# First modulation sums two tiles at a time, one statistic product, and x loaded into the slots of the residual sums

## The chip, the cores and the metric

The kernel runs on one core of a Trainium2 chip. The metric is device time in microseconds (us); smaller is better. The core's engines are TensorE (PE; its weight loads are shown as PEld), VectorE (DVE), ScalarE (ACT), GpSimd (POOL) and SyncE (SP), which here only issues DMA transfers.

## What is computed

Two network blocks over 512 tokens of width 1024, in float32. Only the first matters here:

```python
c_act = jax.nn.silu(c)
mod = c_act @ ada_w[l] + ada_b[l]
shift, scale, gate = jnp.split(mod, 3, axis=-1)
h = rmsnorm(x, norm_g[l]) * (1.0 + scale[:, None, :]) + shift[:, None, :]
p = h @ w_in[l]
y_rwkv = rwkv7_group(p[..., :RWKV_COLS], ...)      # 8 heads
y_sb = stick_breaking_group(p[..., RWKV_COLS:], sb_norm_g[l])   # 8 heads
y = jnp.concatenate([y_rwkv, y_sb], axis=-1) @ w_out[l]
x = x + gate[:, None, :] * y
return rmsnorm(x, final_g)
```

The second block (a short convolution layer, then a neighbourhood attention layer, each with a feed-forward part, over these tokens and 256 context tokens) follows and is not touched.

## The kernel before

Activations lie feature by token: x is eight tiles of 128 features x 512 tokens. A float32 product with a weight is made of three fp32r products: each operand is split into a high part (a rounded copy, made on ACT) and a low part (the difference, made on DVE), and hi x hi, lo x hi and hi x lo are summed in PSUM (mm3, lines 172 to 174). A weight is loaded by SP into a slot "st" (two slots), split into wh and wl (lines 155 and 156; four slots each), and used. So an output tile of a product over six k tiles is 18 PE instructions, over eight 24.

**The head** (block1, lines 310 to 371). SP loads x as four pairs of tiles (512 KB each). The mean square of x (sumsq, lines 250 to 264) is made so: ACT squares the tiles, DVE adds the squares of tiles 0 to 5 into one, PE sums that over the features with a product by a constant matrix, and adds the squares of tiles 6 and 7 with two more such products; these are plain float32 products. Then rsqrt (lines 240 to 248): Ln and Exp on ACT. The modulation vector, shift and scale of all eight tiles, comes from c (cc, a small load on ACT's queue, then a tanh on ACT, line 331) and the 1024 x 2048 matrix ada_n, in four chunks of 512 columns. A chunk is loaded by SP in four transfers of two k tiles (512 KB, line 344). Each k tile is one product with a stationary operand of 32 columns, placed in one of four column groups of the array (line 348), so that four partial sums arise side by side in one PSUM bank. ACT copies the bank out (ev, line 350), four products with a selecting column add the four groups and turn the row into columns (line 353), and DVE adds the bias (line 356). Chunk 0 holds the scale of tiles 0 to 3, chunk 1 the shift of tiles 0 to 3, chunk 2 the scale and chunk 3 the shift of tiles 4 to 7. After a scale chunk the gain is made (line 359), after a shift chunk four tiles are modulated (modulate: nt on DVE at line 287, the high part h on ACT at 289, the low part on DVE at 290).

Between the chunks SP also loads the first halves (k tiles 0 to 3) of five weight tiles of w_in: 12 and 0 after chunk 1, 4 and 8 after chunk 2, 13 after chunk 3. Their products over k 0 to 3 start ahead, each in a PSUM bank of its own (banks ss, acc, acc, sc, so); those over k 4 to 7 follow when tiles 4 to 7 of h are there. "The five tiles" below are these.

**The middle.** Four pairs of RWKV heads (rwkv_pair) and four pairs of stick-breaking heads (sb_pair) are interleaved. An sb pair works through four query blocks of 128, two heads each: scores (line 1147), a mask (1148), two sigmoids on ACT (sg and om, 1151 and 1152), a running product on DVE (cum, 1156), a product (sg, 1158), transposes on PE (1162), a copy (pt, 1164), and products with v (so, 1169); then a norm (osq 1172, its product 1174, ors). Scores and transposes of all blocks share one PSUM bank (ss), so the eight steps of an sb pair are a chain. The modulation vectors of gate and of the next layers are made by DVE as a filler (line 210).

**Block 1's end** (lines 393 to 468). When the y tiles are there, each is split into h (lines 306 and 307, "split"), in the order YORD = (0, 4, 1, 5, 2, 6, 3, 7). Before the last two, the products with w_out over the first six (k 0 to 5) are made for eight outputs m: for m = 0 to 5 the sum "part" = x + gate * product is written over a slot of y that is free by then (lines 419 to 423), for m = 6 and 7 the product stays in PSUM. The bank "acc" has two slots, so the third product waits for the first part. The x tiles of these sums (xt, line 404) are loaded by SP into a pool "tail" that is opened after the last sb pair and lies over space of the RWKV pool; on SP's queue they stand ahead of the eight loads of the context (xc, line 407). The context is normed and modulated there as well (hc). Last come the products over the y tiles 3 and 7 (w_out2, line 448), the new x, and its statistics.

The order of the instructions on each engine's queue is not written out: a planner fixes it when the program is built, from the order in the text, priorities (high_priority raises one) and its own estimates of durations and transfers. On the chip each queue then runs in that order.

## Time and profile before

| | us |
|---|---|
| median of 3 runs | 2110.76 |
| lowest and highest of them | 2107.98, 2111.87 |
| profiled execution, its own time | 2105.49 |
| its span (first to last instruction) | 2103.7 |
| PE busy in it | 2051.8 |
| DVE busy | 1231.9 |
| ACT busy | 795.2 |

The profile shows one execution. A line of its timeline gives start, duration, engine, source line, operation and operands, and in brackets how long the engine was idle before and what ended that. A name before the arrow is what is written, those after it are read; "x5" counts instructions. "PEclk" is the clock that was granted to TensorE, as a share of full speed. PE's busy time is modelled and counts a product at a low clock as busy.

### The profile page before, as it was taken

To read this page: it belongs to the slowest core of one execution; us is meant where nothing else is said; L and a number is where in the kernel's file an instruction comes from. 1 tells how busy PE (TensorE), PEld (TensorE's weight loads), DVE (VectorE), ACT (ScalarE), POOL (GpSimd) and SP (SyncE) were. 2 spreads that over 40 slices of the span, in tenths; PEclk is the share of its full clock that TensorE was granted. 3 is DMA by queue.
4 is the path that set the end of the run, shared out by engine and by line. 5 is a ranking of instruction groups with operands and counts; after the bars stand their busy time and mean duration, and the time that the engine had idled before them with its cause. 6 is when DMAs were issued, how large, how long until landed. Compare 5 with 4: busy or idle time off the path is not lost.

```text
span 2103.7 us, 33543 instructions
## 1 busy us (share of the span) xinstructions
PE 2051.8 (98%) x13596; PEld 1651.6 (79%) x13596; DVE 1231.9 (59%) x2641; ACT 795.2 (38%) x1485; POOL 131.5 (6%) x212
## 2 busy tenths in 40 slices
PE   6999999998999999999999999999999999999999
PEld 3766666655888888888888888898777787888887
DVE  2969887645777756767456443354566655434443
ACT  3536444345422224221222122244777744323232
POOL 0000000000000000001001000000233200000000
PEclk9999999987999999999999999999999999999999
DMA  7432313112243421445234322222111122333333
GB/s 279 147 111 83 111 53 98 40 56 81 71 129 122 130 81 45 147 127 174 90 123 155 114 91 60 61 81 71 43 59 61 36 66 92 95 100 96 94 99 102
DMA packets 61356, 203.60 MB, mean 97 GB/s; under 512 B 6928, under 2 KB 8976, under 8 KB 61200
## 3 DMA queue, kind: packets, MB, share of 16 engines
q1 hardware_dynamic: 45360, 145.77, 21.3%
q0 software_dynamic: 15120, 55.06, 8.1%
q8 instruction: 107, 1.75, 0.3%
q10 hardware_dynamic: 720, 0.62, 0.1%
q14 instruction: 49, 0.40, 0.1%
HBM read 199.32 MB, written 2.10 MB: 96 GB/s over the span
## 4 chain that ended last, share of the span: by engine, by line
PE 87%; ACT 3%; DVE 3%; issue 1%; POOL 0%; POOLq 0%; ACTq 0%; DVEq 0%
PE acc L173 19%; PE acc L172 19%; PE acc L174 19%; PE cacc L174 5%; PE cacc L173 5%; PE cacc L172 5%; PE py L895 2%; PE pT L875 2%; PE ss L1147 1%; PE so L1169 1%; PE sm L862 1%; PE py L1083 1%; PE sm L863 1%; PE py L1081 1%; PE ss L1162 1%
## 5 line engine op out<-in xcount | busy, mean ns | idle before, releaser
L155 ACT CAST wh<-st 128x512 fp32r<-128x512 f32 (+2 forms) x481 | 292.3, 609 | 729.8 <-PE acc L173 287.7
L156 DVE TENSOR_TENSOR wl<-st,wh 128x512 fp32r<-128x512 f32 (+2 forms) x481 | 323.1, 674 | 353.9 <-ACT wh L155 350.7
L172 PE MATMUL acc<-xzzh,wh 128*128 128x512 f32 x352 | 138.8, 394 | 0.0
L174 PE MATMUL acc<-xzzh,wl 128*128 128x512 f32 x352 | 138.1, 392 | 0.0
L173 PE MATMUL acc<-xzzl,wh 128*128 128x512 f32 x352 | 138.0, 392 | 0.0
L210 DVE CUSTOM_DVE_ANT_0 junk<-ast,cb,vec 128x512 bf16<-128x512 f32 x168 | 125.2, 745 | 14.5 <-DMA ast<-in_w_ada_dram 11.9
L210 DVE CUSTOM_DVE_ANT_0 junk<-ast,cb,m 128x512 bf16<-128x512 f32 x168 | 125.5, 747 | 2.8
L200 POOL DMA_DIRECT2D ast<-in_w_ada_dram x96 | 50.6, 528 | 1022.3 <-DVE m L210 957.2
L174 PEld LDWEIGHTS acc<-xzzh,wl 128*128 128x128 f32 x352 | 66.0, 188 | 14.8
L172 PEld LDWEIGHTS acc<-xzzh,wh 128*128 128x128 f32 x352 | 66.1, 188 | 13.6 <-issue 0.5
L173 PEld LDWEIGHTS acc<-xzzl,wh 128*128 128x128 f32 x352 | 66.1, 188 | 13.4 <-issue 0.5
L172 PE MATMUL acc<-h0h,wh 128*128 128x512 f32 (+1 forms) x164 | 65.8, 401 | 6.0 <-DVE part L421 3.1
L173 PE MATMUL cacc<-czzl,wh 128*128 128x256 f32 x240 | 68.1, 284 | 0.0
L172 PE MATMUL cacc<-czzh,wh 128*128 128x256 f32 x240 | 67.7, 282 | 0.0
L174 PE MATMUL cacc<-czzh,wl 128*128 128x256 f32 x240 | 67.3, 280 | 0.0
L174 PE MATMUL acc<-h2h,wl 128*128 128x512 f32 (+1 forms) x164 | 65.8, 401 | 0.0
L173 PE MATMUL acc<-h1l,wh 128*128 128x512 f32 (+1 forms) x164 | 65.7, 401 | 0.0
L173 PE MATMUL acc<-h3l,wh 128*128 128x512 f32 (+1 forms) x164 | 65.3, 398 | 0.3 <-DVE h3l L290 0.3
L173 PE MATMUL acc<-h6l,wh 128*128 128x512 f32 (+1 forms) x164 | 65.5, 399 | 0.1
L173 PE MATMUL acc<-h0l,wh 128*128 128x512 f32 (+1 forms) x164 | 65.4, 399 | 0.0
L174 PE MATMUL acc<-h0h,wl 128*128 128x512 f32 (+1 forms) x164 | 65.3, 398 | 0.1
L174 PE MATMUL acc<-h1h,wl 128*128 128x512 f32 (+1 forms) x164 | 65.2, 398 | 0.0
(731 smaller groups left out, 5576.1 us busy)
## 6 DMA issues: line engine op xcount, KB each, us to landing
ast<-in_w_ada_dram POOLq DMA_DIRECT2D x96, 512.0 KB, 3.8
st<-in_ffn_w_in_dram SPq DMA_DIRECT2D x88, 512.0 KB, 3.4
st<-in_ffn_w_out_dram SPq DMA_DIRECT2D x32, 448.0 KB, 3.3
st<-in_w_in_dram SPq DMA_DIRECT2D x24, 512.0 KB, 3.5
st<-in_conv_w_in_dram SPq DMA_DIRECT2D x24, 512.0 KB, 3.6
ast<-in_ada_n_dram SPq DMA_DIRECT2D x16, 512.0 KB, 9.0
st<-in_ffn_w_out_dram SPq DMA_DIRECT2D x16, 512.0 KB, 3.5
st<-in_w_qk_dram SPq DMA_DIRECT2D x16, 512.0 KB, 3.5
```

Of the source, the lines that this page charges most:

```text
L155: nc.scalar.copy(hi[:, :n], sl)
L156: nc.vector.tensor_tensor(lo[:, :n], sl, hi[:, :n].bitcast(F32), ALU.subtract)
L172: mm(out, lhsT=lh, rhs=rh, start=first, stop=False)
L173: mm(out, lhsT=lh, rhs=rl, start=False, stop=False)
L174: return mm(out, lhsT=ll, rhs=rh, start=False, stop=last)
L200: self.nc.gpsimd.dma_start(st, src)
L210: i = self.nc.vector.tensor_tensor_reduce(out=junk, in0=st[:, hs], in1=c[:, hs], scale=0.5, scalar=o if hf else self.V(bname, j), op0=ALU. ...
L862: mm(o, lhsT=qh[:, e, qs], rhs=ks, start=True, stop=False)
L863: mm(o, lhsT=ql[:, e, qs], rhs=ks, start=False, stop=True)
L875: nc.tensor.transpose(pT[:, to], s[:, 128 * i:128 * i + 128], self.C("ident"))
L895: self.nc.tensor.matmul(po[r, cs], lhsT=v[:, r], rhs=pts[e][:, blk:blk + n].rearrange("p a t -> p (a t)"), start=i == 0, stop=i == len(wor ...
L1081: mm(o, lhsT=SV[e][:, c], rhs=MMt[e][:, c], start=True, stop=c == 0)
```

## The change

- The sums of the first modulation: a chunk now holds the scale of two tiles (256 columns) and their shift (256 columns), so that after each of the four chunks two tiles of h are modulated. A chunk is loaded in two transfers of four k tiles (1 MB) instead of four of two (512 KB), and each transfer gives four products, one per column group. The columns are rearranged on the host. ev has slots of its own.
- The five early weight tiles are loaded one chunk sooner: 12 and 0 after chunk 0, 4 and 8 after chunk 1, 13 after chunk 2.
- The statistic of x: DVE adds all eight squares and one product follows, instead of five adds and three products. Its result lies in bank "so" and no longer in "sm", which the modulation's columns use.
- cc is a constant tile and its load is the first on ACT's queue.
- The Exp of every rsqrt is planned at high priority.
- x for the residual sums of block 1: the six extra tiles in "tail" are gone. When y[k] has been split, an x tile is loaded into the slot of y[k], and the sum is written in place.

```diff
--- before.py
+++ after.py
@@ -96,6 +96,8 @@
     def build(self):
         nc, tc, A = self.nc, self.tc, self.A
         cp = self.cp = self.pool("const")
+        self.cc = cp.tile([128, 8], F32, name="cc")
+        nc.scalar.dma_start(self.cc, A["ccol"])
         self.vec = cp.tile([128, NVEC], F32, name="vec")
         nc.scalar.dma_start(self.vec, A["vec"])
         self.con = cp.tile([128, 384], F32, name="con")
@@ -245,19 +247,20 @@
         if since is not None:
             self.order(i, since)
         src, dst = (t, t) if out is None else (view[1](t), view[0](out))
-        return nc.scalar.activation(dst, src, AF.Exp, scale=-0.5)
-
-    def sumsq(self, xs, n, pool, tag, psum, scale=None):
+        with self.tc.high_priority():
+            return nc.scalar.activation(dst, src, AF.Exp, scale=-0.5)
+
+    def sumsq(self, xs, n, pool, tag, psum, scale=None, direct=2):
         nc = self.nc
         acc = pool.tile([128, n], F32, tag=tag + "cs", name="acc")
         sc = lambda k: 1.0 if scale is None else scale[:, k:k + 1]
         first = nc.scalar.activation(acc, xs[0], AF.Square, scale=sc(0))
-        for k in range(1, 6):
+        for k in range(1, KT - direct):
             sq = pool.tile([128, n], F32, tag=tag + "z", name="sq")
-            nc.scalar.activation(sq, xs[k], AF.Square, scale=sc(k))
+            first = nc.scalar.activation(sq, xs[k], AF.Square, scale=sc(k))
             nc.vector.tensor_add(acc, acc, sq)
-        nc.tensor.matmul(psum, lhsT=self.C("ones"), rhs=acc, start=True, stop=False)
-        for k in (6, 7):
+        nc.tensor.matmul(psum, lhsT=self.C("ones"), rhs=acc, start=True, stop=direct == 0)
+        for k in range(KT - direct, KT):
             sq = pool.tile([128, n], F32, tag=tag + "z", name="sq")
             first = nc.scalar.activation(sq, xs[k], AF.Square, scale=sc(k))
             nc.tensor.matmul(psum, lhsT=self.C("ones"), rhs=sq, start=False, stop=k == 7)
@@ -325,42 +328,39 @@
             xs = [x2[k // 2][:, k % 2] for k in range(KT)]
             for k in range(KT // 2):
                 nc.sync.dma_start(x2[k], A["x"][k])
-            cc = npool.tile([128, 8], F32, name="cc", bufs=1)
-            nc.scalar.dma_start(cc, A["ccol"])
             ct = npool.tile([128, 8], F32, name="ct", bufs=1)
-            nc.scalar.activation(ct, cc, AF.Tanh, scale=0.5)
+            nc.scalar.activation(ct, self.cc, AF.Tanh, scale=0.5)
             cp32 = npool.tile([128, 8, 32], F32, name="cp32", bufs=1)
             b32 = lambda t: t.unsqueeze(2).to_broadcast([128, 8, 32])
-            nc.vector.scalar_tensor_tensor(cp32, b32(ct), 1.0, b32(cc), op0=ALU.add, op1=ALU.mult)
-            ps = self.psum("sm")
-            first = self.sumsq(xs, S, npool, "n", ps)
+            nc.vector.scalar_tensor_tensor(cp32, b32(ct), 1.0, b32(self.cc), op0=ALU.add, op1=ALU.mult)
+            ps = self.psum("so")
+            first = self.sumsq(xs, S, npool, "n", ps, direct=0)
             rstd = npool.tile([128, S], F32, tag="nzc", name="rstd")
             self.rsqrt(rstd, ps, first)
             tr = self.psum("sm")
             for ch in range(4):
                 pm = self.psum(("py", "sp")[ch % 2])
-                for kp in range(4):
-                    st = npool.tile([128, 2, 512], F32, tag="ast", name="ast", bufs=16)
-                    nc.sync.dma_start(st, A["ada_n"][ch, kp])
-                    for i in range(2):
-                        k = 2 * kp + i
-                        r = slice(32 * (k % 4), 32 * (k % 4) + 32)
-                        nc.tensor.matmul(pm[r], lhsT=cp32[:, k], rhs=st[:, i], start=k < 4, stop=k >= 4)
-                ev = npool.tile([128, 512], F32, tag="nz", name="ev")
+                for kh in range(2):
+                    st = npool.tile([128, 4, 512], F32, tag="ast", name="ast", bufs=8)
+                    nc.sync.dma_start(st, A["ada_n"][ch, kh])
+                    for i in range(4):
+                        r = slice(32 * i, 32 * i + 32)
+                        nc.tensor.matmul(pm[r], lhsT=cp32[:, 4 * kh + i], rhs=st[:, i], start=kh == 0, stop=kh == 1)
+                ev = npool.tile([128, 512], F32, tag="ev", name="ev")
                 nc.scalar.copy(ev, pm)
-                j = (8, 0, 12, 4)[ch]
                 for i in range(4):
-                    nc.tensor.matmul(tr[:, j + i:j + i + 1], lhsT=ev[:, 128 * i:128 * i + 128], rhs=self.C("sel"),
-                                     start=True, stop=True)
-                mj = self.m1[:, j:j + 4, 0]
-                nc.vector.scalar_tensor_tensor(mj, tr[:, j:j + 4], 0.5, self.V("ada_b", j, 4),
+                    nc.tensor.matmul(tr[:, 4 * ch + i:4 * ch + i + 1], lhsT=ev[:, 128 * i:128 * i + 128],
+                                     rhs=self.C("sel"), start=True, stop=True)
+                k0 = 2 * ch
+                mg, ms = self.m1[:, 8 + k0:10 + k0, 0], self.m1[:, k0:k0 + 2, 0]
+                nc.vector.scalar_tensor_tensor(mg, tr[:, 4 * ch:4 * ch + 2], 0.5, self.V("ada_b", 8 + k0, 2),
                                                op0=ALU.mult, op1=ALU.add)
-                if j >= 8:
-                    nc.vector.scalar_tensor_tensor(g1[:, j - 8:j - 4], mj, 1.0, self.V("norm_g", j - 8, 4),
-                                                   op0=ALU.add, op1=ALU.mult)
-                else:
-                    self.modulate(xs, range(j, j + 4), g1, self.m1, 0, 0, h, npool, "nz", rstd)
-                for t, tag in ((), ((12, "ss"), (0, "acc")), ((4, "acc"), (8, "sc")), ((13, "so"),))[ch]:
+                nc.vector.scalar_tensor_tensor(g1[:, k0:k0 + 2], mg, 1.0, self.V("norm_g", k0, 2),
+                                               op0=ALU.add, op1=ALU.mult)
+                nc.vector.scalar_tensor_tensor(ms, tr[:, 4 * ch + 2:4 * ch + 4], 0.5, self.V("ada_b", k0, 2),
+                                               op0=ALU.mult, op1=ALU.add)
+                self.modulate(xs, range(k0, k0 + 2), g1, self.m1, 0, 0, h, npool, "nz", rstd)
+                for t, tag in (((12, "ss"), (0, "acc")), ((4, "acc"), (8, "sc")), ((13, "so"),), ())[ch]:
                     st = npool.tile([128, 512], F32, tag="wst", name="wst", bufs=5)
                     nc.sync.dma_start(st, W[t][:, :512])
                     wst.append((t, tag, st))
@@ -399,9 +399,6 @@
                 for k in range(8):
                     nc.sync.dma_start(A['dbg_y'][k], y[k])
             with self.open(name="tail", bufs=2) as tp:
-                xts = [tp.tile([128, S], F32, name=f"xt{m}", bufs=1) for m in range(6)]
-                for m in range(6):
-                    nc.sync.dma_start(xts[m], A["x"][m // 2, :, m % 2])
                 xc = self.xc = [self.cxp.tile([128, SC], F32, tag=f"xc{k}", name=f"xc{k}") for k in range(KT)]
                 for k in range(KT):
                     nc.sync.dma_start(xc[k], A["ctx"][k])
@@ -417,10 +414,8 @@
                     if k == 3:
                         for m in range(6):
                             po = self.xgemm(A["w_out"][m], yh, 0, 6)
-                            t = self.yp.tile([128, S], F32, tag=f"y{YORD[m]}", name="part")
-                            nc.vector.scalar_tensor_tensor(t, po, self.m1[:, 16 + m, 0:1], xts[m],
+                            nc.vector.scalar_tensor_tensor(part[m], po, self.m1[:, 16 + m, 0:1], part[m],
                                                            op0=ALU.mult, op1=ALU.add)
-                            part.append(t)
                         for m in (6, 7):
                             po = self.psum("acc")
                             self.gemm(po, A["w_out"][m], yh, 0, 6, last=False)
@@ -429,6 +424,11 @@
                     t = self.hl(self.hp, S, f"h{k}")
                     self.split(t, y[k])
                     yh.append(t)
+                    m = len(part)
+                    if m < 6:
+                        t = self.yp.tile([128, S], F32, tag=f"y{k}", name="part")
+                        nc.sync.dma_start(t, A["x"][m // 2, :, m % 2])
+                        part.append(t)
         xs = self.xs = [xa.tile([128, S], F32, tag=f"x{k}", name=f"x{k}") for k in range(KT)]
         for k in (6, 7):
             nc.sync.dma_start(xs[k], A["x"][k // 2, :, k % 2])
@@ -1231,7 +1231,8 @@
     o["con"] = make_consts()
     o["ada_w"] = np.ascontiguousarray(f["ada_w"][0][:, 2 * D:].T).reshape(8, 128, D)
     o["ada_n"] = np.ascontiguousarray(
-        f["ada_w"][0][:, :2 * D].reshape(4, 2, 128, 4, 512)[:, :, :, [2, 0, 3, 1]].transpose(3, 0, 2, 1, 4))
+        f["ada_w"][0][:, :2 * D].reshape(2, 4, 128, 2, 4, 256)[:, :, :, ::-1].transpose(4, 0, 2, 1, 3, 5)
+        .reshape(4, 2, 128, 4, 512))
     o["ccol"] = np.ascontiguousarray(f["c"][0].reshape(KT, 128).T)
     o["cvec"] = np.stack([f["c"][0], f["c_2"][0], f["c_ctx_2"]])
     w = f["w_in"][0]
```

## The prediction

> **What bounds the kernel now.** I read the page first, then the busy time by windows, then the timeline and waits of the two stretches that the edits touch.

> ```profile
> span 2103.7 us, 33543 instructions
> PE 2051.8 (98%) x13596; PEld 1651.6 (79%) x13596; DVE 1231.9 (59%) x2641; ACT 795.2 (38%) x1485; POOL 131.5 (6%) x212
> PEclk9999999987999999999999999999999999999999
> ```

> PE is counted busy almost throughout, so time is won only where PE starts late, runs products of small use, or runs at a low clock. The clock row dips in one place, slices 9 and 10 (about 420 to 525 us). The windows (columns: stretch, length, PE, PEld, DVE, ACT, POOL busy, granted clock, DMA share, GB/s):

> ```profile
> 4.50:36.00 31.50, 19.92 (x78) 7.89 (x78) 11.80 (x24) 12.94 (x21) 0.66 (x1) 0.89 1.02 401
> ...
> 26.30:33.30 7.00, 6.31 (x13) 1.69 (x13) 5.06 (x8) 2.53 (x4) 0.00 (x0) 0.55 1.03 403
> 33.30:69.80 36.50, 36.00 (x157) 23.76 (x155) 19.98 (x48) 16.11 (x26) 3.90 (x8) 0.99 0.46 141
> ...
> 453.00:489.00 36.00, 26.77 (x110) 12.80 (x110) 12.73 (x30) 14.19 (x25) 0.00 (x0) 0.56 0.32 99
> 489.00:524.40 35.40, 35.00 (x143) 25.98 (x144) 24.16 (x54) 16.73 (x34) 0.00 (x0) 0.87 0.19 57
> 524.40:540.30 15.90, 14.20 (x56) 9.84 (x54) 14.33 (x23) 8.35 (x14) 0.00 (x0) 1.00 0.28 97
> ```

> Two soft places. The head loads at 401 GB/s with all queues full until 36 us, and then PE works without a hole to 69.8. Block 1's end (453 to 540.3) has PE idle and at a clock of 0.56. Clock times busy time there is 26.77 x 0.56 + 35.00 x 0.87 + 14.20 = 59.7 us of work in 87.3 us: 27.6 us is the most that could be won at this place.

> **The head, part by part.**

> ```profile
> ACT ct L331 <- DMA cc<-in_ccol_dram: 3.5, 1, 3.5
> ```
> ```profile
> 9.78 3.88 DVE L258 TENSOR_TENSOR acc<-acc,sq 128x512 f32<-128x512 f32 x5
> 13.71 2.07 PE L259 MATMUL sm<-acc,con 128*128 128x512 f32 x2 [13.71 <-DVE acc L258]
> 15.57 2.48 PE L263 MATMUL sm<-sq,con 128*128 128x512 f32 x4
> 17.98 1.92 PE L348 MATMUL py<-ast,cp 128*32 128x512 f32 x16
> 22.23 0.75 DVE L287 SCALAR_TENSOR_TENSOR nt<-x,gain,rstd 128x512 f32<-128x512 f32 x1
> 25.55 0.72 ACT L289 ACTIVATE h0h<-nt,m 128x512 fp32r<-128x512 f32 x1 [0.82 <-DVE m L356]
> 26.33 0.50 PE L172 MATMUL ss<-h0h,wh 128*128 128x512 f32 x1 [1.01 <-ACT h0h L289]
> ```

> Today the tanh of c holds ACT for 3.5 us ahead of the squares; with cc first on its queue that wait shrinks to between 0 and 3.5. Seven adds instead of five cost 7 x 0.776 = 5.4 us; they end between 11.7 (start 3.5 us sooner) and 15.2 (no sooner). I take 12, because x is first on SP's queue, as cc now is on ACT's. One statistic product replaces three: 2.07 us, to 14.1, where today the third ends at 18.05. Chunk 0's products stand right behind (17.98). Their data, 2.1 MB behind 2.1 MB of x, takes 4.2 MB / 401 GB/s = 10.5 us, by 15.0 at the latest even if it began only at 4.5. So they run at about 14.5, 3.5 us sooner, for 1.92 us.

> Today h0 also waits for the shift in chunk 1. From the end of chunk 0's products (19.90) to the first nt (22.23) pass 2.3 us; with nt and h0h that is 3.8. In the new order chunk 0 holds scale and shift of tiles 0 and 1, so the first weight product moves from 26.33 to 14.5 + 1.9 + 3.8 = 20.2: 6.1 us sooner.

> What is done on PE from then on:

> ```profile
> 37.03 0.40 PE L172 MATMUL ss<-h3h,wh 128*128 128x512 f32 x1
> 37.35 1.05 PE L348 MATMUL py<-ast,cp 128*32 128x512 f32 x4
> 38.34 0.50 PE L173 MATMUL ss<-h3l,wh 128*128 128x512 f32 x1
> ...
> 69.55 0.39 PE L174 MATMUL so<-h7h,wl 128*128 128x512 f32 x1
> ```

> A load of two k tiles, dropped between weight products, spreads two starts to 38.34 - 37.03 = 1.31 us, 1.08 over the usual 0.23 (six products of w_out start 0.23 apart below, too). Chunks 2 and 3 have eight such loads today, four of four k tiles in the new kernel. Four col groups side by side cost about what two do (17.98: eight products in 1.92), so 4 x 1.08 = 4.3 us go. But chunk 1, which today lies before 26.33, now falls among the products: two loads and its transposing products, 3 x 1.08 = 3.2. Net 1.1 us. Head: 6.1 + 1.1 = 7.2, **taken as 7 us** at the end of the five tiles (69.94), if PE is fed and the next stage starts sooner by it. Bounds: 0 (fed as late as today) and 10 (the half clock of 26.3 to 33.3, worth 7.0 x 0.45 = 3.2, goes as well).

> [...]

> **Block 1's end.** Here the x loads matter.

> ```profile
> L306 ACT CAST h0h<-y x1: 622/622/622, 421.0 to 421.0; 128x512 fp32r<-128x512 f32 x1
> L306 ACT CAST h6h<-y x1: 622/622/622, 435.1 to 435.1; 128x512 fp32r<-128x512 f32 x1
> ```
> ```profile
> SPq L167 <- DVE wl L156: 30.2, 3, 18.7
> SPq L404 <- DVE tb L1099: 22.4, 1, 22.4
> ```
> ```profile
> 452.01 0.40 PE L174 MATMUL acc<-h6h,wl 128*128 128x512 f32 x1
> 488.51 0.72 DVE L421 SCALAR_TENSOR_TENSOR part<-acc,m,xt 128x512 f32<-128x512 f32 x1
> 489.29 0.79 PE L172 MATMUL acc<-h0h,wh 128*128 128x512 f32 x1 [3.07 <-DVE part L421]
> 496.75 0.69 DVE L1158 TENSOR_TENSOR sg<-sg,cum 128x512 f32<-128x512 f32 x1
> 499.32 0.60 PE L1162 MATMUL ss<-con,sg 128*128 128x128 f32 x4
> 507.78 0.62 ACT L306 CAST h7h<-y 128x512 fp32r<-128x512 f32 x1 [0.42 <-DVE y L1180]
> 518.39 0.68 DVE L307 TENSOR_TENSOR h7l<-y,h7h 128x512 fp32r<-128x512 f32 x1
> 524.47 0.39 PE L172 MATMUL acc<-h3h,wh 128*128 128x512 f32 x1
> ```
> ```profile
> 489.00:524.40 35.40, 14.63 (x36) 7.30 (x36) 0.87 0.19 57
> ```

> By 452.4 two w_out outputs fill both acc banks. The sums that empty them (part, L421) come at 488.51 and after, because their x goes to a pool over the space of rwkv pair 3: SP waits 22.4 us there, and the order was planned around late x. Behind them stand 3 x 36 = 108 products (the last row counts one line of three, L174), 108 x 0.23 = 24.8 us of work, while PE idles at 0.56. Only then come the products with h3 and h7 (524.47), although h7 could be split from 507.78.

> In the new kernel x goes where y was, free once y is split: 421 to about 436.5 (435.1 + 0.62 + 0.68). The new wait stands on SP; behind it are w_out's and the context's loads. The w_out load already waits up to 18.7 us for a weight slot, so a wait ending at 436.5 delays nothing, and x landing late could cost a part one load. The 108 products can then fill 453 to 508. If pair 3's chain keeps its time, the last products start at 507.78 + 0.62 + 0.68 = 509.1: 15.4 us sooner. If the chain also shortens, more, up to the 27.6 of PE's work. How it runs beside products shows sb pair 2, from its third score product to its norm product, against pair 3:

> ```profile
> 397.34 0.91 PE L1147 MATMUL ss<-qk,qk 64*128 64x384 f32 x2
> ...
> 425.38 1.02 PE L1174 MATMUL ss<-osq,con 128*128 128x512 f32 x2
> ...
> 459.60 1.64 PE L1147 MATMUL ss<-qk,qk 64*128 64x384 f32 x2
> ...
> 502.97 1.02 PE L1174 MATMUL ss<-osq,con 128*128 128x512 f32 x2
> ```

> 28.0 us in a full stretch against 43.4 in the empty, cold one. So it will shorten, but the context's work and DVE (24.16 of 35.40 us at 489 to 524.4) then meet it. **I take 18 us**, nearer to 15.4.

> **At nothing.** In two places a sigmoid stands between Ln and Exp; the second:

> ```profile
> 475.86 0.69 ACT L242 ACTIVATE Z<-rsm,epsb 128x512 f32<-128x512 f32 x1 [0.86 <-PE rsm L1093]
> 476.56 1.28 ACT L1152 ACT_TABLE_LOAD   x1
> 477.86 0.49 ACT L1152 ACTIVATE om<-ss 128x384 f32<-128x384 f32 x1
> 478.37 1.28 ACT L248 ACT_TABLE_LOAD   x1
> 479.66 0.63 ACT L248 ACTIVATE Z<-Z 128x512 f32<-128x512 f32 x1
> ```

> With Exp at high priority two of three table loads go (2.6 us of ACT) and Exp comes 3.1 us sooner, but om, on pair 3's chain, comes 0.6 later (476.55 + 0.63 + 1.28 = 478.46). The w_out products that now fill this stretch hide both; without them it is -3 to +1 us. The second evacuation buffer (ev) and cc's new pool move no work.

> **Sum.** The profiled execution took 2105.49 us, 1.79 around its span: 2105.5 - 7 - 18 = 2080.5. It lies 5.3 below the median of the runs, 2110.76; the 25 us are taken off the median: **2085.8**.

> **Rivals.**
> *B, tail alone.* The first weight products come in bursts between chunks, and PE runs them at half clock, as at 26.3 to 33.3 (0.55). From 20.2 to 33.3 that is 13.1 x 0.45 = 5.9 us lost instead of 3.2; with h2 and h3 late on top, the 7 are gone: 2110.8 - 18 = 2092.8. [...] Against B: tiles 12 and 0 alone offer 12 products, and more weights land with each chunk.

> *C, head alone.* The planner leaves the w_out products behind pair 3's chain although x is there; then 2110.8 - 7 = 2103.8. For it: the order on PE and DVE is fixed ahead, and nothing in the trace shows how it was costed. Against: two w_out outputs were already planned among the chain, before the banks were full.

> *E, nothing:* both steps fail to change the order, 2110.8.

> *F, slower.* The freed products stand ahead of pair 3's chain on PE's in-order queue. From 459.6 the chain comes to PE 13 times (three per block of four, and the norm). At pair 2's pace h7 would be due at 507.8 - 15.4 = 492.4; break-even with today lies at 507.8 + 15.4 + 7 = 530.2, 2.9 us per visit. A whole output of 18 products each time is 4.1 us: 15.6 us slower, 2126. Against it: the transposes at 499.32 waited 1.9 us behind such products (sg was done at 497.44), under 2.9, and pair 2 ran well.

> **The numbers.** Both gains 0.53 (its own range 2073 to 2096, from the bounds), tail alone 0.18, head alone 0.13, nothing 0.06, slower 0.10. Range 2073 to 2105: 10 + 27.6 off at the low end, and C at the high end; nothing and F stay outside. A change of 0.2%, 4.2 us, is about what a measurement of this kernel can tell from none. Faster is A, B and C, 0.84.

> **What would show it.** The first weight product near 20, the five tiles done near 63; the first part sum before 460; a clock near 1.0 from 453 to 489; products with h3 and h7 starting about 25 us sooner than 524.47. Wrong if PE still shows holes at 0.56 there, if SP waits long at the x loads, or if pair 3's norm product comes later than 503.

## The result, and the profile after

The changed kernel takes 2091.74 us in the median (2089.64 to 2098.8, four runs), the kernel before in the same session 2109.37 us (four runs): a ratio of 0.9926, 95% interval [0.9901, 0.9952]. The forecast was 2085.8 us in a range of 2073 to 2105, 25 us less than before; measured are 17.6 less. Six more runs of the changed kernel in a later session had a median of 2098.97 us, 0.9937 [0.9913, 0.996] of the kernel before beside them (10.5 us less); the section on experiments shows by what the two sets of runs differ. The profiled run took 2090.8 us. From its page:

```profile
span 2089.0 us, 33529 instructions
...
PE 2039.2 (98%) x13592; PEld 1647.7 (79%) x13592; DVE 1234.4 (59%) x2649; ACT 796.9 (38%) x1487; POOL 131.1 (6%) x212
...
PEclk9999999999999999999999999999999999999999
```

The dip in slices 9 and 10 of the clock row is gone. The busy time by windows, in the same stretches as before (PE, PEld, DVE, ACT, POOL busy, granted clock, DMA share, GB/s):

```profile
4.50:36.00 31.50, 16.35 (x72) 8.06 (x73) 12.96 (x29) 12.41 (x22) 0.66 (x1) 0.89 1.00 402
26.30:33.30 7.00, 6.96 (x30) 3.16 (x29) 0.84 (x2) 0.74 (x2) 0.00 (x0) 0.75 1.00 408
33.30:69.80 36.50, 35.67 (x167) 24.65 (x168) 23.10 (x58) 17.54 (x28) 4.01 (x8) 0.95 0.45 152
453.00:489.00 36.00, 35.72 (x186) 22.45 (x187) 22.07 (x49) 20.02 (x39) 0.00 (x0) 1.00 0.26 81
489.00:524.40 35.40, 30.34 (x122) 21.78 (x120) 28.32 (x56) 19.13 (x36) 0.00 (x0) 0.90 0.23 72
524.40:540.30 15.90, 15.90 (x93) 14.00 (x92) 15.50 (x30) 8.51 (x14) 0.00 (x0) 1.00 0.11 34
```

At block 1's end PE went from 26.77 us at a clock of 0.56 to 35.72 us at 1.00 in the first of the three stretches. The loads of 1 MB brought no more bandwidth to the head: 402 GB/s after 401. The sums that waited for x now run from 442.0 on, where before they began at 488.51, and x itself lands within 3.7 us of its issue (the rows of their two lines: duration min/median/max in ns, first and last start):

```profile
L417 DVE SCALAR_TENSOR_TENSOR part<-acc,m,part x6: 744/751/752, 442.0 to 492.2; 128x512 f32<-128x512 f32 x6
```
```profile
L430 SPq DMA_DIRECT2D part<-in_x_dram x6: 327/334/1133, 429.5 to 436.1; - x6
...
DMA to landing us min/median/max: 2.5/3.2/3.7
```

SP does wait long at the first of these loads, for the split of y[0]:

```profile
SPq L430 <- DVE h0l L310: 23.7, 1, 23.7
```

This delays nothing on PE: from 400 to 430 us it is busy for 28.99 of 30 us, as before (29.02), and from 430 to 453 us all the time.

To see where the 14.7 us of span came from, both timelines are cut at the same instructions: the last product of the five tiles, pair 0's second score product, and the statistics product (L461) behind block 1's last sum. Before:

```profile
7.06 0.23 DVE L121 CAST bcon<-con 128x128 bf16<-128x128 f32 x1 [1.71 <-DMA con<-in_con_dram]
8.85 0.23 DVE L122 CAST bcon<-cst 128x128 bf16<-128x128 f32 x1 [1.56 <-DMA cst<-in_con_dram]
...
137.30 0.49 PE L1147 MATMUL ss<-qk,qk 64*128 64x128 f32 x2
...
536.74 1.12 PE L461 MATMUL ss<-acc,con 128*128 128x512 f32 x2 [0.45 <-DVE acc L459]
```

After:

```profile
8.20 0.23 DVE L123 CAST bcon<-con 128x128 bf16<-128x128 f32 x1 [1.46 <-DMA con<-in_con_dram]
...
10.35 0.23 DVE L124 CAST bcon<-cst 128x128 bf16<-128x128 f32 x1 [1.59 <-DMA cst<-in_con_dram]
10.49 5.87 DVE L261 TENSOR_TENSOR acc<-acc,sq 128x512 f32<-128x512 f32 x7
...
16.42 2.08 PE L262 MATMUL so<-acc,con 128*128 128x512 f32 x2 [16.42 <-DVE acc L261]
18.43 2.47 PE L348 MATMUL py<-ast,cp 128*32 128x512 f32 x16
...
25.14 0.79 PE L174 MATMUL ss<-h0h,wh 128*128 128x512 f32 x1 [2.47 <-ACT h0h L292]
...
67.72 0.39 PE L176 MATMUL so<-h7h,wl 128*128 128x512 f32 x1
...
138.88 0.48 PE L1147 MATMUL ss<-qk,qk 64*128 64x128 f32 x2
...
494.40 1.02 PE L1174 MATMUL ss<-osq,con 128*128 128x512 f32 x2
...
502.31 0.39 PE L174 MATMUL acc<-h3h,wh 128*128 128x512 f32 x1
...
507.40 0.68 DVE L310 TENSOR_TENSOR h7l<-y,h7h 128x512 fp32r<-128x512 f32 x1
...
508.14 0.80 PE L175 MATMUL acc<-h7l,wh 128*128 128x512 f32 x1 [3.86 <-DVE h7l L310]
...
521.89 1.12 PE L461 MATMUL ss<-acc,con 128*128 128x512 f32 x2 [0.16 <-DVE acc L459]
```

Lengths of the stages in the profiled runs, in us, with two of the experiments below for comparison:

| stage | before | changed | tail only | changed, second profile |
|---|---|---|---|---|
| start to five tiles done | 69.94 | 68.11 | 70.04 | 69.78 |
| to pair 0's second score product | 67.36 | 70.77 | 68.60 | 79.53 |
| to the statistics product L461 | 399.44 | 383.01 | 379.04 | 382.45 |
| to the end | 1566.96 | 1567.11 | 1568.92 | 1566.84 |
| span | 2103.7 | 2089.0 | 2086.6 | 2098.6 |

The head won 1.8 us, the stage behind it gave back 3.4, and block 1's end won 16.4. The net gain is no more than what block 1's end won.

### The profile page after: what moved, and what is told of

The parts are those of the page before. It is cut to its first block, busy times and chain, and to the rows that moved or that the text cites. A ratio compares the mean times of both kernels' runs of the same rounds, so it can differ in the third digit from the quotient of the medians.

```text
span 2089.0 us, 33529 instructions
## 1 busy us (share of the span) xinstructions
PE 2039.2 (98%) x13592; PEld 1647.7 (79%) x13592; DVE 1234.4 (59%) x2649; ACT 796.9 (38%) x1487; POOL 131.1 (6%) x212
## 4 chain that ended last, share of the span: by engine, by line
PE 87%; DVE 3%; ACT 3%; issue 1%; POOL 0%; POOLq 0%; ACTq 0%; DVEq 0%
PE acc L175 20%; PE acc L174 19%; PE acc L176 19%; PE cacc L176 5%; PE cacc L175 5%; PE cacc L174 5%; PE py L895 2%; PE pT L875 2%; PE ss L1147 1%; PE sm L862 1%; PE so L1169 1%; PE sm L863 1%; PE py L1083 1%; PE py L1081 1%; PE G L979 1%
## 5 line engine op out<-in xcount | busy, mean ns | idle before, releaser
L174 PE MATMUL acc<-xzzh,wh 128*128 128x512 f32 x352 | 138.8, 394 | 0.0
L174 PEld LDWEIGHTS acc<-xzzh,wh 128*128 128x128 f32 x352 | 66.1, 188 | 13.4 <-issue 0.5
L174 PE MATMUL acc<-h0h,wh 128*128 128x512 f32 (+1 forms) x164 | 66.5, 406 | 3.0 <-DVE fs L643 3.0
L175 PE MATMUL acc<-h7l,wh 128*128 128x512 f32 (+1 forms) x164 | 65.4, 399 | 3.9 <-DVE h7l L310 3.9
L174 PE MATMUL cacc<-czzh,wh 128*128 128x256 f32 x240 | 67.7, 282 | 0.0
L176 PE MATMUL cacc<-czzh,wl 128*128 128x256 f32 x240 | 67.2, 280 | 0.0
L174 PE MATMUL acc<-h3h,wh 128*128 128x512 f32 (+1 forms) x164 | 65.3, 400 | 0.8 <-DVE x L451 0.8
L176 PE MATMUL acc<-h3h,wl 128*128 128x512 f32 (+1 forms) x164 | 65.6, 400 | 0.0
L175 PE MATMUL acc<-h5l,wh 128*128 128x512 f32 (+1 forms) x164 | 65.6, 400 | 0.0
L176 PE MATMUL acc<-h4h,wl 128*128 128x512 f32 (+1 forms) x164 | 65.5, 400 | 0.0
```

What stands on the lines that cost most here:

```text
L174: mm(out, lhsT=lh, rhs=rh, start=first, stop=False)
L175: mm(out, lhsT=lh, rhs=rl, start=False, stop=False)
L176: return mm(out, lhsT=ll, rhs=rh, start=False, stop=last)
```

## Experiments

### The tail alone, and the head alone

The first kernel is the one before with only the x loads moved:

```diff
-                xts = [tp.tile([128, S], F32, name=f"xt{m}", bufs=1) for m in range(6)]
...
+                    m = len(part)
+                    if m < 6:
+                        t = self.yp.tile([128, S], F32, tag=f"y{k}", name="part")
+                        nc.sync.dma_start(t, A["x"][m // 2, :, m % 2])
```

> Before, with only x loaded into the slots of y; the head and the Exp priority are as before. Theory T (the whole gain comes from the w_out products freed between 453 and 489, and what the head wins is lost before the first attention block): 13 to 19 us faster than before, as much as the whole change or a little more, since the planned order here has the split of h7 (L307) right behind the first context split instead of behind all eight: products with h3 near 503, the last products with h7 not held, statistics product of the next block (L458 here) at 515 to 521. Rival U (the slots need the earlier head or the Exp priority to be planned well): under 8 us faster.

It took 2090.02 us, 0.9907 [0.9894, 0.992] of before, 19.7 us less (13 to 19 expected), so it is as fast as the whole change. Its products with h7 follow those with h3 at once, without the hole of 3.86 us:

```profile
502.62 0.39 PE L172 MATMUL acc<-h3h,wh 128*128 128x512 f32 x1
...
503.52 0.39 PE L173 MATMUL acc<-h7l,wh 128*128 128x512 f32 x1
...
517.68 1.12 PE L461 MATMUL ss<-acc,con 128*128 128x512 f32 x2 [0.23 <-DVE acc L459]
```

The second kernel is the changed one with x loaded into the old pool.

```diff
+                xts = [tp.tile([128, S], F32, name=f"xt{m}", bufs=1) for m in range(6)]
+                for m in range(6):
+                    nc.sync.dma_start(xts[m], A["x"][m // 2, :, m % 2])
...
-                        nc.sync.dma_start(t, A["x"][m // 2, :, m % 2])
```

> The changed kernel with x loaded into the old pool over pair 3's space again; head edits and Exp priority stay. Theory T: within 3 us of before (first weight product near 25, third score product of pair 0 within 1.5 us of before's 157.46, clock again near 0.56 from 453 to 489). Rival V (the head edits are worth what was forecast, 7 us, and another part of the change costs some of it back): 5 to 8 us faster than before.

It took 2107.44 us, 0.9988 [0.9973, 1.0002]; PE is idle and at a low clock again at block 1's end:

```profile
453.00:489.00 36.00, 26.99 (x121) 13.56 (x119) 14.59 (x33) 13.35 (x23) 0.00 (x0) 0.63 0.31 99
```

Its twelve runs fall into two groups, six of 2099.7 to 2105.9 us at a granted clock of 0.985 to 0.988 and six of 2109.0 to 2113.4 at 0.981 to 0.983. So the x loads make the gain by themselves, theory U and rival V fall, and the head is worth nothing in the median, though something in half of the runs.

### What holds the sums of squares

In the changed kernel tanh of c is early (4.68) and so are the first squares, but the adds start at 10.49, behind two casts into bcon on DVE's queue, and these wait for constants. One edit takes the casts off that queue:

```diff
-            nc.vector.tensor_copy(self.bcon[:, 0:128], self.C("ident"))
-            nc.vector.tensor_copy(self.bcon[:, 128:256], st[:, :128])
+            nc.gpsimd.tensor_copy(self.bcon[:, 0:128], self.C("ident"))
+            nc.gpsimd.tensor_copy(self.bcon[:, 128:256], st[:, :128])
```

> The changed kernel with the two casts into bcon moved from DVE to GpSimd. Theory T1 (the seven adds wait behind these two casts on DVE's queue, and the casts wait for their loads): adds start near 6.5 instead of 10.49, end near 12.5, statistic product near 12.5 instead of 16.42, first weight product near 21 instead of 25.14; the five tiles done 2 to 4 us sooner than 67.72. In the whole time 0 to 4 us faster than the changed kernel, nearer to 0 if what the head wins is lost before 158 as it was. Rival W (the adds are late because x lands late): adds start at 10 or later as well, nothing moves.

```profile
7.01 5.91 DVE L261 TENSOR_TENSOR acc<-acc,sq 128x512 f32<-128x512 f32 x7
...
12.98 2.07 PE L262 MATMUL so<-acc,con 128*128 128x512 f32 x2 [12.98 <-DVE acc L261]
14.98 3.13 PE L348 MATMUL py<-ast,cp 128*32 128x512 f32 x16
...
22.36 0.79 PE L174 MATMUL ss<-h0h,wh 128*128 128x512 f32 x1 [2.47 <-ACT h0h L292]
```

The adds run 3.5 us sooner and the five tiles are done at 64.93, 3.2 sooner than after and 5.0 sooner than before. T1 holds, W falls. Yet the time is 2092.48 us, 0.9913 [0.99, 0.9927]: nothing of it reaches the end.

### Where the head's gain goes: the clock between the five tiles and pair 0's scores

The busy time in that stage, for the kernel before, the changed one, its second profile, and the one with the casts moved:

```profile
69.94:137.30 67.36, 62.47 (x948) 48.04 (x948) 52.90 (x121) 29.05 (x55) 4.22 (x8) 0.97 0.40 133
```
```profile
68.11:138.88 70.77, 64.67 (x949) 49.18 (x949) 53.13 (x120) 29.64 (x56) 4.22 (x8) 0.95 0.40 126
```
```profile
69.78:149.31 79.53, 71.74 (x949) 54.14 (x948) 53.26 (x121) 29.54 (x56) 4.50 (x9) 0.85 0.35 115
```
```profile
64.93:144.71 79.78, 72.06 (x949) 53.65 (x949) 52.98 (x120) 29.64 (x56) 4.22 (x8) 0.85 0.35 113
```

These are the same products. Length times granted clock is 65.3, 67.2, 67.6 and 67.8 us: counted at full clock the stage takes 65 to 68 us, and the two long ones are those that were granted less of the clock. The second profile comes from running the changed kernel once more:

> The changed kernel once more, unchanged. Theory T4: its stage from the five tiles to pair 0's second score product may take another length than the 71.2 us of its first profile (68 to 80), and length times granted clock is again 67 within 1 us; the other stages repeat within 1 us. Rival: the stage repeats within 1 us, and the longer stages of the other kernels come from their edits.

Its stage took 79.53 us instead of 70.77 with not one instruction changed, while the third and fourth stages repeated within 0.6 us. T4's sum holds; that holes of PE bring the half clock is seen only in the order of events. The ten runs of the changed kernel fall into five of 2089.6 to 2093.8 us at a clock of 0.992 or 0.993, and five of 2098.8 to 2104.3 at 0.988 to 0.990; the first session caught more of the one, the second more of the other. In the second profile the clock falls three times, each time in or behind a hole of PE: from 76.75 to 80.0 us behind a wait of 2.97 us for ACT, and twice more, as its PE timeline and its windows show:

```profile
104.60 0.69 PE L1002 MATMUL pQ<-XZ,Uc 32*32 32x32 f32 x57
108.00 0.33 PE L1002 MATMUL pQ<-XZ,Uc 32*32 32x32 f32 x7 [2.71 <-issue]
...
118.94 0.25 PE L1014 MATMUL pQ<-XZ,U 32*32 32x32 f32 x3 [1.03 <-issue]
```
```profile
108.00:114.00 6.00, 6.00 (x150) 5.42 (x149) 4.25 (x9) 0.00 (x0) 0.53 (x1) 0.50 0.19 42
114.00:116.00 2.00, 2.00 (x85) 1.76 (x75) 0.60 (x2) 0.62 (x1) 0.00 (x0) 0.95 0.98 338
116.00:120.00 4.00, 2.86 (x46) 2.40 (x46) 1.72 (x4) 2.58 (x5) 0.00 (x0) 1.00 0.44 172
120.00:134.00 14.00, 14.00 (x79) 10.47 (x78) 6.62 (x13) 3.10 (x9) 0.53 (x1) 0.54 0.24 76
```

"Issue" means that PE waited for nothing that the profile shows: no semaphore, no data. The hole opens within a row of 64 tiny products, after 57 of them.

Read in windows of 0.25 us, the stretches near half clock between 66 and 140 us last 3.25 to 3.5, 6.75 to 7.0, 13.75 or 17.25 us in all fourteen profiles: one, two, four or five steps of about 3.4 us. Within a profile they also start a whole number of such steps apart (second profile: 76.75, 107.25 and 121.0; first: 105.0 and 132.25). How a hole lies to these steps differs from execution to execution: in the first profile the half clock began 0.9 us behind the end of the hole of 2.71 us (104.05), in the second 0.6 us ahead of it (108.0). The stretches of 13.75 and 17.25 us stand in five profiles (this one, the casts on GpSimd, and below h7 first, Exp plain and the first of the three edits), all of runs at 0.988 to 0.990, each behind a second hole of 1.0 to 1.3 us. The two other profiles of these kernels, at 0.992, have the first hole of 2.71 us, but neither the second one nor the long stretch.

### Three edits together, and one wait less

Two further suspects were tried singly first. The products with h7 wait because the split of h7 stands behind the whole context modulation on DVE, so this split was put at high priority:

```diff
-                    self.split(t, y[k])
+                    if k == 7:
+                        with tc.high_priority():
+                            self.split(t, y[k])
+                    else:
+                        self.split(t, y[k])
```

> The changed kernel with the split of the last output tile of block 1's gated norm (h7) at high priority. Theory T2 (the products with h7 wait for DVE, where the split of h7 stands behind the whole context modulation): h7l done near 502 instead of 508, no hole of 3.86 us ahead of the first product with it, the next block's statistics product at 514 to 518 instead of 521.89, and 4 to 7 us faster than the changed kernel. Rival X (the context's products or the sums behind take the place of that wait): the statistics product at 520 or later, within 2 us of the changed kernel.

```profile
513.16 0.39 PE L175 MATMUL acc<-h7l,wh 128*128 128x512 f32 x1
...
517.95 0.50 PE L174 MATMUL acc<-h3h,wh 128*128 128x512 f32 x1 [2.82 <-DVE x L455]
```

The hole ahead of h7l is gone, but one of 2.82 us for the sums behind stands in its place. From the first product with h3 to the statistics product it takes 16.8 us instead of 19.6 in the changed kernel: 2.8 won where 4 to 7 were expected, and rival X has part of it: this hole, and one step of half clock behind it (519.5 to 522.75). The time, 2093.65 us or 0.9926 [0.9914, 0.9937], is that of the changed kernel; this profile's stage behind the five tiles fell to a clock of 0.85 as well.

Then Exp without its priority:

```diff
-        with self.tc.high_priority():
-            return nc.scalar.activation(dst, src, AF.Exp, scale=-0.5)
+        return nc.scalar.activation(dst, src, AF.Exp, scale=-0.5)
```

> The changed kernel without the high priority of Exp. In the four kernels with it, pair 2's norm product comes 2.4 to 3.3 us sooner after pair 0's second score product than in the two without, and pair 3's first score product then comes 3.9 later: net 1 us at most. Theory T3 (the priority is worth nothing, and only moves work about): these two shifts vanish, from pair 0's second score product to the next block's statistics product 380 to 384 us against 383.0, and the time is within 3 us of the changed kernel. Rival Y (the priority saves its table loads on the path): 3 to 5 us slower than the changed kernel.

2095.07 us, 0.9923 [0.99, 0.9946]: the same as the changed kernel, as forecast. But the two shifts stayed (pair 3's first score product still comes 10.9 us behind pair 2's norm product, 6.9 before), so they are not Exp's doing and T3 was wrong there. The order that the planner finds turns over with edits elsewhere: in the kernel of the next but one experiment it is 6.9 again. The two shifts cancel to less than 1 us.

All three edits, the casts on GpSimd, h7 first and Exp plain:

> The changed kernel with three edits together: casts of bcon on GpSimd, h7's split at high priority, Exp plain. Five tiles done near 64.5 (67.7 in the changed kernel), no hole ahead of the products with h7, statistics product 25 us after pair 3's norm product (27.5). Theory T4 (what the head wins is lost between the five tiles and pair 0's second score product because short holes of PE there halve the clock): that stage takes 67 us of full clock whatever the kernel, so its length is 67 divided by the granted clock; with a clock of 0.85 to 0.98 it takes 68 to 79 us, and the whole time is 2084 to 2093. Rival Z (the stage is bound by loads that land at fixed times, not by the clock): length times clock falls well under 67 there.

2089.89 us, 0.9898 [0.9872, 0.9924]. Three runs took 2082.0 to 2085.0 us at a clock of 0.992 to 0.995, three 2094.8 to 2096.2 at 0.988. The profile is one of the latter: five tiles done at 65.33, then 78.71 us at 0.85, 66.9 of full clock. T4's sum holds again, Z falls.

Next, the second lora product in a bank of its own, so that PE needn't wait there for a sigmoid:

```diff
-        pw, pa = self.psum("sp"), self.psum("sp")
+        pw, pa = self.psum("sp"), self.psum("ss" if p == 0 else "sp")
```

> As the kernel with the three edits, and in pair 0 the second lora product (pa) goes to the free bank ss instead of waiting in sp for the first one's sigmoid. Theory T4: the hole of 0.8 to 2.6 us ahead of that product (L930) is gone, the clock in 68 to 80 us is at or above 0.95 (0.73 in the kernel with the casts on GpSimd), and the stage loses the 2 to 5 us that the hole and the half clock behind it cost; 2 to 5 us faster than with the three edits alone if the other holes (L1002, L1014) stay as they are. Rival Z2: another hole takes its place a few products later, clock and time stay within 2 us.

```profile
PE sp L948 <- ACT t L935: 5.0, 1, 5.0
```

The wait moved to the next product that needs the bank sp and is longer there (5.0 us against 2.1 at L933 with the three edits). 2091.12 us, 0.9902 [0.9884, 0.9921]: no gain, rival Z2.

### Feeding PE's instruction stream

The hole of 2.7 us has a companion in the DMA traffic: in the second profile of the changed kernel the instruction queue moves one packet at 105.7 to 105.8 us, with PE at rest from 105.3 to 108.0.

```profile
q8 instruction: 1, 0.02, 58.2%
```

In the first profile it comes at 101.7 and PE goes on at 104.05, with the three edits at 100.4 and 102.72: each time 2.3 us pass from the packet to the next product. It is so throughout: the fourteen profiles have 21 holes of over 0.6 us between 90 and 120 us that end in "issue", and each ends 2.2 to 2.7 us behind a packet of this queue. A reading of the author's, which no profile shows: PE had run out of code. Then a few slower products among the tiny ones (they took 0.5 us each, the tiny ones 12 ns) would give the code time. They compute nothing that is used:

```diff
             pQ = bank("pQ")
+            for _ in range(2 if p == 0 else 0):
+                mm(pQ[:, 1], lhsT=self.C("ones"), rhs=X, start=True, stop=True)
```

With four, and with two:

> The kernel with the three edits, and in pair 0 four extra products of 128x256 ahead of each of the four rounds of 64 tiny products (16 in all, into a half bank that nobody reads). They need 4 instructions for about 1 us of PE and so slow the rate at which PE uses up its code there. Theory T5 (the hole of 2.7 us at the tiny products, which ends 2.3 us behind a 16 KB packet of the instruction queue, is PE out of code, and it and the hole of 1.0 behind it bring the half clock of 100 to 130 us): the holes shrink below 1 us, the clock there stays at 1.0 in the profile, the stage from the five tiles to pair 0's second score product takes 68 to 71 us, no run lies near the 2095 that three of six runs of the three edits took, all at 2083 to 2087. Rival Z3 (the holes and the clock do not hang on the rate of code): half the runs near 2095 plus 4, the others near 2082 plus 4.

> As the kernel before with two extra products instead of four ahead of each round (8 in all, 2.1 us of PE). Theory T5: the holes shrink by about half of what four do, some runs still fall into the long half clock; median between 2083 and 2090. Rival Z3: two clusters as with the three edits, each later by 2 us.

With two, the waits of PE and the windows:

```profile
PE pQ L1007 <- issue: 0.9, 1, 0.9
```
```profile
100.00:135.00 35.00, 32.85 (x550) 24.65 (x548) 25.33 (x63) 14.75 (x33) 2.11 (x4) 1.00 0.40 128
```

and the same windows with the three edits alone:

```profile
100.00:135.00 35.00, 31.16 (x380) 23.97 (x378) 17.08 (x40) 10.06 (x23) 1.58 (x3) 0.71 0.30 95
```

The hole shrinks from 2.7 to 0.9 us, the clock in this window is 1.00, and all five runs lie within 2.4 us (2087.38 to 2089.75, clock 0.993 to 0.996): median 2088.43, 0.9905 [0.989, 0.9919]. T5 had expected that some runs still fall into the long half clock, and none did; but with the three edits alone eight of twelve runs lie above 0.990 as well, so five runs don't show that it is gone.

With four the longest hole of this kind is 0.5 us and the clock is 1.00 in the same window too, but the kernel takes 2098.32 us, 0.9951 [0.9937, 0.9965], 11 us over the upper end of what T5 expected, and three of its six runs have a clock of 0.990 or less. The clock row of its profile (a slice is 52.5 us) dips in the slice that begins at 262 us:

```profile
PEclk9999989999999999999999999999999999999999
```

There PE waits 3.03 us for DVE, until 301.88, and the clock is 0.50 from 302.75 to 323.25, which costs 10 us; the order of the products differs too, with pair 0's first two score products 8.4 us apart instead of 25.1. Ahead of a row the four products take 1.9 us (103.15 to 105.07) where about 1 was expected, so the 16 are some 7.5 us, an estimate. So T5 holds for the length of the holes. That PE was out of code in them, and that the clock follows from them, isn't shown: here the half clock came behind another hole, one of data. With two products a gain isn't shown either: the median lies 1.5 us under that of the three edits alone (2089.89), well within the spread of its runs.

### Is it the head that brings the long half clock?

> The tail-only kernel once more. So far its four runs took 2088 to 2094 at a granted clock of 0.992 to 0.994, while half of the runs of the kernels with the new head fell to 0.988 to 0.990 and took 5 to 13 us more. Theory T6 (the old head meets the tiny products of pair 0 at a moment at which the long half clock does not follow): again all runs at 0.991 or more, within 6 us. Rival (four runs were luck): a third or more of the runs at 0.990 or less and at 2096 or more.

> The kernel with the three edits once more. Theory T6: again two groups of runs, near 2082 to 2085 at 0.992 to 0.995 and near 2095 at 0.988, and a median within 3 us of the tail-only kernel run beside it, though its head is 4.7 us sooner. Rival: the slower group does not come again, and the median lies 5 us or more under the tail-only kernel's.

Tail only: 2088.53 us, 0.9909 [0.9894, 0.9923]. The three edits: 2088.24 us, 0.9905 [0.9887, 0.9923], this time with one run of six at 0.990. Over both sessions all eight runs of the tail-only kernel have a clock of 0.992 to 0.995 and lie between 2086.4 and 2093.3 us; of the 38 runs of the five kernels with the new head, the slots and no other edit of pair 0, 16 have 0.990 or less. So T6 is borne out in part: the medians lie 0.3 us apart and the tail-only kernel stays above 0.991, but the two groups of the three edits did not come again, as the rival had it. Nor does the old head escape the holes: in the two profiles of the tail-only kernel they take 1.29 and 2.72, and 1.64 and 1.36 us, with 3.5 and 7.0 us at half clock behind them; only the long stretch is missing. The fastest runs of all are those of the three edits at full clock (2082), but in the median they equal the tail alone. Both lie about 19 us under the kernel before, and in the median under the changed kernel too (2091.74 and 2098.97), though the intervals of those ratios overlap.

## Why the prediction came out as it did

The number lies 6 us under the result and well within the range, but the result is the one that rival B named (tail alone, 2092.8). The range held every outcome from both gains at their most to the head alone, so that it was met says nothing of the head; in the later session the changed kernel took 2098.97 us.

*Bounds.* Right. The soft place at 453 to 524 us was where time could be won, and the gain stayed under the 27.6 us given as the most.

*The squares.* This step failed: "they end between 11.7 (start 3.5 us sooner) and 15.2 (no sooner). I take 12". They ended at 16.4, outside both bounds. The working looked at what ACT waits for and not at what stands ahead of the adds on DVE. cc now goes first on ACT's DMA queue, and vec, con and cst behind it are issued 0.4 to 0.7 us later and land 1.1 to 1.5 us later (the casts at 8.20 and 10.35 instead of 7.06 and 8.85); the adds stand behind these casts. No run moves cc alone, so that its place is the whole cause of the later landing is not shown. The larger part was there before: the second cast stood at 8.85 and the adds could not have begun sooner, only the tanh, late as well (9.02), hid it. With the casts moved, the adds ended at 12.9, the chunk's products started at 14.98 (forecast 14.5), the first weight product came at 22.36 (forecast 20.2, mostly as the chunk's products took 3.13 us instead of 1.92), and the five tiles were done at 64.9 (forecast 63). From the first weight product, 4.0 us sooner than before, to the end of the tiles, 5.0 sooner, it won the 1.1 us that the prediction had given to fewer loads.

*"Head: taken as 7 us at the end of the five tiles, if PE is fed and the next stage starts sooner by it."* 1.8 and 0.2 us in the two profiles (in the second the later cast came at 11.66 instead of 10.35). In the first, the squares, 4.4 us behind the forecast, are most of the 5.2 us that are missing. The condition failed besides: even the 5.0 us of the kernel with the casts moved were lost by pair 0's scores. Rival B named the half clock, but in the wrong place, and not the squares. It put the loss at 20 to 33 us; of that stretch, 26.3 to 33.3 ran at 0.75 after 0.55. The clock was lost at 68 to 140.

*The x loads.* Right in what they free: the sums start at 442, the 108 products fill the stretch, pair 3's chain from the third block's score product to its norm product shortens from 43.4 to 33.1 us (461.31 to 494.40, the norm product before at 502.97), and F, which had it later, falls. A long wait of SP at these loads was named as a sign of being wrong; it came (23.7 us) and delayed nothing on PE, so the sign was badly chosen.

*"I take 18 us."* 16.4 in the changed kernel, 20.4 with the tail alone. The products with h3 came 22.2 us sooner, in the upper part of the bounds of 15.4 and 27.6. Of that 7.3 us went again until L461 (19.6 us instead of 12.3): "the context's work and DVE then meet it" was the right worry, and the split of h7 behind the context's modulation was its place: the hole of 3.86 us ahead of h7l, and behind it two steps of half clock (507.75 to 514.5), which cost 3.4. Put first, the split won 2.8 of them; the tail-only kernel, with neither, takes 15.1 us there.

*Exp at nothing.* Right; the two kernels can't be told apart.

## What to carry to other kernels

When an edit brings a load forward, list what it passes on its DMA queue and which in-order engine then waits for those loads: here the load of c went ahead of the constants, and the work that it was to free stood behind these. A stage that starts sooner is worth only what the stages behind it pass on, so look there for holes of PE and for the granted clock before adding the gain to the sum, and where a kernel's runs form two groups, compare clock against time for each run before comparing medians. Test an edit of several parts one part at a time: here one part carried all of the gain.
